# Strassen pairs of a down projection: T's weight sum on VectorE in place of transfers, all pairs one feed-forward block later, the product banks' folds moved back

## The chip, the cores and the metric

The kernel runs on one core of one Trainium2 chip. The metric is the device time of one execution in microseconds (us). The engines are TensorE (PE in the profile, with its weight loads as PEld), VectorE (DVE), ScalarE (ACT), GpSimd (POOL) and SyncE (SP). SP and POOL also issue transfers (DMAs) between HBM and SBUF; only POOL's transfers can add what they bring to what is already in SBUF.

## The reference

A trunk of two layers on one sequence of 256 tokens with 1024 features, all in float32. Each layer has a token mixer and a SwiGLU feed-forward network. The change lies in the feed-forward network of the second layer, which is the end of the program:

```
def swiglu(h, w13, w2):
    g, u = jnp.split(h @ w13, 2, axis=-1)
    return ((jax.nn.silu(g) * u) @ w2).astype(h.dtype)

for layer in range(DEPTH):
    ...
    h = h + y
    h = h + swiglu(rms_norm(h, norm_ffn[layer]), ffn_w13[layer], ffn_w2[layer])
return rms_norm(h, final_norm)
```

`w13` has 1024 rows and 2 x 2816 columns, `w2` has 2816 rows and 1024 columns. In blocks of 128, the hidden dimension of 2816 is 22 blocks.

## The kernel before

**Precision.** Float32 operands are handed to TensorE as two parts. ScalarE rounds a piece to its high part (`whi`, line 448, for weights), VectorE subtracts that from the piece to get the low part (`wlo`, line 450). A product is then three matmuls: high by high, high by low, low by high. A piece of weights is up to 128x1024 elements. These two instructions are called its split below. Products of activations (`xh`/`xl`, `hh`/`hl`) are split in the same way.

**Weights.** They are laid out ahead in one array, in the order in which they are used (`weight_plan`). SP loads a segment of 128x1024 (512 KB) into a ring of buffers called `raw`; two more buffers of this ring lie in the tile `bt`, which is free by then, so in this stage it holds 8.

**The feed-forward network of the second layer.** Block j (0 to 21) of the hidden dimension takes 48 matmuls (`gate_up`): 8 input blocks by gate and up by three. From block 4 on all of them write one PSUM bank, half gate, half up. `hidden1` then lets ScalarE apply silu to the gate half (`sgq`, line 1434) and VectorE multiply the up half by it (`uu`, line 1449; `u`, line 1455, for the last blocks). The next block may write that bank only after this.

**Strassen pairs.** The first 18 of 22 row blocks of the down projection are taken two at a time, in 9 pairs (`QUADS`), by Strassen's scheme: seven products in place of eight, each summed over all pairs in a PSUM bank of its own, `m7[1]` to `m7[7]` (1, 2, 3, 5 shown as psA, 4, 6, 7 as psB). The weights of a pair are two segments, a = [A | B] and b = [C | D]. Four pieces are made of them:

- "D" is A - B, a VectorE subtraction (`wdiff`, line 486);
- the plain piece is a itself;
- "S" is b + a, made by a POOL transfer of 512 KB that adds a's data from HBM into b's buffer (line 475);
- "T" is [A + D | B + C], made by two POOL transfers of 256 KB that add b's halves, swapped, into a's buffer, once a's own split has read it.

When the odd block of a pair is there, `combine` makes the four activation operands. `early(p)` then runs products 1, 2 and 5 (pieces D and a, 9 matmuls), `late(p)` products 3 and 4 (piece S) and 6 and 7 (piece T), 12 matmuls. Blocks 4 to 21 are followed by these halves in turn: block 4 + 2p by early(p), block 5 + 2p by late(p). The last 4 row blocks of the down projection are plain matmuls in `Final`, into four of the same banks, and then residual, norm and output.

**Folds.** After the last pair, VectorE adds each product bank into the result `ht` with the sign and place that Strassen's scheme gives it (`fold`, line 1500). All folds read and write `ht`, so they run in the order in which they were created: banks 2, 5, 5, 1, 1, 3, 4, 4. `Final`'s first part writes into bank 3, another into bank 2, each after that bank's fold.

**Order.** The program hands operations to a list scheduler with an engine, a cost and a due time, counted in tiles of TensorE's work. The scheduler sets each engine's order by these, and the engine then runs its instructions strictly in that order. The pieces of weights are made in the order of a list, `subs`; S and T of a pair are entered in it a given number of segments after the pair's own (`then`). A buffer that is `held` is not given back to its ring until its last split.

Of the kernel before, what the change touches and what calls it, by code (L numbers as in the profile page):

```python
# [16 lines left out]
S = 256  # L17
D = 1024
# [23 lines left out]
def weight_plan():  # L42
# [28 lines left out]
    def ffn(layer):  # L71
        for k in range(KT - 2):
            for j in range(4):
                plan.append(("ffn_w13", layer, k, P * j, P))
                plan.append(("ffn_w13", layer, k, DFF + P * j, P))
        for j in range(4):
            for half in range(2):
                column("ffn_w13", layer, half * DFF + P * j, (KT - 2, KT - 1))

        for j in range(4, FTN):  # L80
            column("ffn_w13", layer, P * j)
            column("ffn_w13", layer, DFF + P * j)
            if layer == 0:
                rows("ffn_w2", layer, j - 4)
            elif j % 2 == 0:
                plan.extend(quad(j - 4))
        if layer == 0:
            for k in range(FTN - 4, FTN - 2):
                rows("ffn_w2", layer, k)
            last_rows("ffn_w2", layer, FTN)  # L90
        else:
            for k in range(FTN - 4, FTN):
                for nh in range(2):
                    plan.append(("ffn_w2", layer, k, 512 * nh, 512))
# [216 lines left out]
def hybrid_trunk(ctx: ExitStack, tc: tile.TileContext, wts, xT, par, gfin, tab, onehot, masks, out):  # L311
# [98 lines left out]
    for si, (_, n) in enumerate(segs):  # L410
        if si in quads:
            add_sub("D", si, 0, 512, 2)
            add_sub("", si, 0, SUB, 4)
            then = [3, si]
        elif si - 1 not in quads:
            for o in range(0, n, grain(si)):
                m = min(grain(si), n - o)
                add_sub("", si, o, m, m // P)
        if then:
            then[0] -= 1  # L420
            if then[0] < 0:
                add_sub("S", then[1] + 1, 0, SUB, 4)
                add_sub("T", then[1], 0, SUB, 4)
                then = []
# [4 lines left out]
    def make_subs(upto):  # L429

        while ws["made"] < min(upto, len(subs)):
# [4 lines left out]
                quad_sums(si, due)  # L436
            elif kind == "" and o == 0 and si not in quads:
                load(si, due)
            src = {"": raws, "D": diffs, "S": raws, "T": raws}[kind][si]
            h = new("whi", [P, SUB], NSUB, FR, held=True)  # L440
            lo = new("wlo", [P, SUB], NSUB, FR, held=True)
            hi_b.append(h)
# [4 lines left out]
            else:  # L447
# [1 line left out]
                      reads=[src], alloc=[h], due=due)  # L449
            ov = od.op("V", cv(n), lambda h=h, lo=lo, r=src, o=o, n=n: V.tensor_tensor(  # L450
                lo[:, :n], r[:, o:o + n], h[:, :n].bitcast(FT), op=OP.subtract), reads=[src, h], alloc=[lo], due=due + .01)
            if not (kind == "" and si in quads):
                src.held = False
            else:
                add_rows(src, (0, 512), si + 1, (512, 0), due + 1)
            if i:
                oa.after, ov.after = ws["A"], ws["V"]
                ws["A"] = oa
# [6 lines left out]
        loads[si] = od.op("S", 60, lambda: nc.sync.dma_start(  # L465
            r[:, :m], wts[c0 // CHUNK, :, c0 % CHUNK:c0 % CHUNK + m]), alloc=[r], nbytes=m * 512, due=due)

    diffs = {}

    def add_rows(b, to, si, frm, due):  # L470

        n = segs[si][0] // CHUNK
        for t, f in ((to[0], frm[0]),) if to == frm else zip(to, frm):
            w = SUB if to == frm else 512
            o = od.op("G", 1000, lambda t=t, f=f, w=w: nc.gpsimd.dma_start(b[:, t:t + w], wts[n, :, f:f + w], accum_op=OP.add),  # L475
                      writes=[b], nbytes=1024 * w, due=due)
            o.deps += b.writers[:1]

    def quad_sums(si, due):

        load(si, due)
        load(si + 1, due)
        a, b = raws[si], raws[si + 1]
        d = diffs[si] = Buf(rings["wdiff"])
        a.held = b.held = True
        od.op("V", cv(512), lambda: V.tensor_tensor(d.tile, a[:, :512], a[:, 512:], op=OP.subtract), reads=[a], alloc=[d],
              due=due - 1)
        add_rows(b, (0, 512), si, (0, 512), due)

    class Piece:  # L490
        def __init__(self, i, c, n):
# [813 lines left out]
    def more_raws():  # L1305

        old, turn = rings["raw"], [0]

        def make():
            turn[0] += 1  # L1310
            n = (turn[0] - 1) % (RAW + 2)
            return bt.tile[:, D * (n + 1):D * (n + 2)] if n < 2 else old.make()
        rings["raw"] = Ring(make, RAW + 2)
        rings["raw"].past = [Buf(None), Buf(None)] + old.past[-RAW:]
    st3 = Stats()
    banks3 = [main_bank("A") for _ in range(4)]
    for k in range(KT):
# [177 lines left out]

    def fold(i, *to):

        for tt, nh, op in to:
            c = slice(512 * nh, 512 * nh + 512)
            read[i] = od.op("V", cv(512), lambda tt=tt, c=c, op=op: V.tensor_tensor(ht[:, tt, c], ht[:, tt, c], m7[i][:, :], op=op),  # L1500
                            reads=[m7[i], ht], writes=[ht], due=2)

    def early(p):
        x = ops[p]
# [5 lines left out]
        for t in "da":  # L1510
            x[t].free()
        if p == QUADS - 1:
            fold(2, (1, 1, OP.subtract))
            fold(5, (0, 1, OP.subtract), (0, 0, OP.add))
            fold(1, (0, 0, OP.add), (1, 1, OP.add))

    def late(p):
        x = ops[p]
# [1 line left out]
        product(p, 3, x["c"], 0, Piece(w.i, 512, 512))  # L1520
        product(p, 4, x["c"], 1, Piece(w.i, 0, 512))
        if p == QUADS - 1:
            fold(3, (1, 1, OP.add))
            fold(4, (0, 0, OP.add), (1, 0, OP.add))
        w = sub_piece("T", SUB)
        product(p, 6, x["b"], 0, Piece(w.i, 0, 512))
        product(p, 7, x["b"], 1, Piece(w.i, 512, 512))
# [8 lines left out]
    for j in range(4, FTN):  # L1536
# [7 lines left out]
        if j == 4:  # L1544
            od.op("A", ca(D), lambda: A.activation(gf.tile, gf.tile, AF.Copy, scale=2 * float(D) ** 0.5), reads=[bt],
                  writes=[gf], due=30)
        (late if j % 2 else early)((j - 4) // 2)
    for k in range(KT):
        x4[k].free()
    final.update({(0, 0): m7[7], (1, 0): m7[3], (0, 1): m7[2], (1, 1): m7[6]})  # L1550
# [4 lines left out]
    for tt in range(2):  # L1555
        fin = Final(tt)
        for i, (nh, o, n) in enumerate(FIN):
            b = final[nh, tt]
            if b in (m7[2], m7[3]):
                od.need(lambda: read[2 if b is m7[2] else 3].end)  # L1560
            for k in ks:
                p = w[k, nh]
                mm_x(b[:, o:o + n], hs[k], Piece(p.i, p.c + o, n), tt, stop=(k == FTN - 1), cost=n / 2.4 + 2.5)
# [54 lines left out]
```

## Time and profile before

| | us |
|---|---|
| three runs | 630.06, 634.36, 635.02 |
| their median | 634.36 |
| the profiled execution, its own time | 633.32 |
| its span in the profile | 631.6 |
| granted TensorE clock over the span | 0.991 |

The span runs from the first to the last instruction of the profiled execution; the 1.7 us beside it lie around it. Times in rows of the profile count from the span's start. The second layer's feed-forward blocks from block 4 on, and with them all that the change touches, lie from about 435 us on. Busy time says how long an engine had an instruction at work, not whether it held anyone up; for that the rows of waits and the chain of work that ended last are read, which name what released each engine. PEclk is the share of full clock that TensorE was granted.

### The profile page before, as it was taken

Reading aid. Unit: us, or ns where it says so; the run is one execution under the profiler, and the core shown is the slowest. Engines: PE = TensorE matmul, PEld = TensorE weight load, DVE = VectorE, ACT = ScalarE, POOL = GpSimd, SP = SyncE. Lnnn points to the kernel's source line nnn. Section 1 sums busy time; section 2 is a strip of 40 time slices with the busy share of each in tenths; the row PEclk is TensorE's granted clock in tenths of the full one; section 3 lists DMA queues with packets and bytes.
Section 4 is the critical chain, followed back from the end, with each engine's and each line's share of the span. In section 5 each row is a group of like instructions: output and inputs, shape, how many; then the busy total and the mean of one; then the engine's idle time right before and its main releaser. Section 6 shows DMA issues by size and latency. Waiting matters only on the chain.

```text
span 631.6 us, 12416 instructions
## 1 busy us (share of the span) xinstructions
PE 610.2 (97%) x4783; PEld 584.6 (93%) x4783; DVE 463.0 (73%) x852; ACT 381.6 (60%) x759; POOL 78.4 (12%) x128
## 2 busy tenths in 40 slices
PE   9999999999999999999999999999899999989985
PEld 7899999999999999999988999999899888988875
DVE  6899997877947666666695788766986666677673
ACT  6799989755635444444475666657855444455543
POOL 0052222000320000000001000004310111111102
PEclk9999999999999999999999999999989999989999
DMA  8855344543998555555526644476468786987911
GB/s 298 336 180 199 136 168 134 168 168 134 194 246 285 198 200 191 184 195 200 200 101 214 220 168 142 159 250 184 101 215 253 203 256 142 313 237 216 249 19 66
DMA packets 37142, 121.93 MB, mean 193 GB/s; under 512 B 4987, under 2 KB 6523, under 8 KB 37084
## 3 DMA queue, kind: packets, MB, share of 16 engines
q1 hardware_dynamic: 31484, 109.05, 50.0%
q0 software_dynamic: 4640, 11.34, 10.8%
q10 hardware_dynamic: 960, 0.76, 0.4%
q8 instruction: 37, 0.61, 0.4%
q14 instruction: 21, 0.17, 0.1%
HBM read 119.76 MB, written 1.38 MB: 192 GB/s over the span
## 4 chain that ended last, share of the span: by engine, by line
PE 59%; issue 25%; DMA 7%; DVE 5%; ACT 2%; POOL 1%; SPq 0%; DVEq 0%; ACTq 0%; POOLq 0%
PE psB L531 37%; PE psA L531 21%; DMA bt<-scr 3%; DVE wlo L450 3%; DMA raw<-in_w_dram 2%; ACT whi L448 1%; DMA bt<-in_w_dram 1%; DMA scr<-be 1%; POOL ny L705 0%; PE psB L1275 0%; ACT u L1414 0%; DVE uu L1449 0%; DVE xl L1419 0%; ACT sgq L1434 0%; POOL u L1416 0%
## 5 line engine op out<-in xcount | busy, mean ns | idle before, releaser
L450 DVE TENSOR_TENSOR wlo<-raw,whi 128x1024 fp32r<-128x1024 f32 (+1 forms) x199 | 237.9, 1206 | 84.1 <-ACT whi L448 84.1
L448 ACT ACTIVATE whi<-raw 128x1024 fp32r<-128x1024 f32 (+1 forms) x198 | 204.3, 1044 | 119.9 <-PE psA L531 49.6
L531 PE MATMUL psB<-xh,whi 128*128 128x256 f32 x608 | 173.7, 289 | 2.8 <-DVE uu L1449 2.8
L531 PE MATMUL psB<-xh,wlo 128*128 128x256 f32 x608 | 168.5, 280 | 0.0
L531 PE MATMUL psB<-xl,whi 128*128 128x256 f32 x608 | 164.0, 280 | 0.0
L531 PE MATMUL psA<-xh,whi 128*128 128x256 f32 x544 | 151.1, 281 | 0.0
L531 PE MATMUL psA<-xh,wlo 128*128 128x256 f32 x544 | 148.7, 277 | 0.0
L531 PE MATMUL psA<-xl,whi 128*128 128x256 f32 x544 | 143.6, 277 | 0.0
L531 PEld LDWEIGHTS psB<-xh,whi 128*128 128x128 f32 x608 | 115.7, 190 | 5.0 <-ACT hh L1464 3.2
L531 PEld LDWEIGHTS psB<-xh,wlo 128*128 128x128 f32 x608 | 115.5, 190 | 0.8 <-DVE wlo L450 0.3
L531 PEld LDWEIGHTS psB<-xl,whi 128*128 128x128 f32 x608 | 113.0, 191 | 0.0
L531 PEld LDWEIGHTS psA<-xh,whi 128*128 128x128 f32 x544 | 102.2, 188 | 0.2
L531 PEld LDWEIGHTS psA<-xh,wlo 128*128 128x128 f32 x544 | 102.3, 188 | 0.0
L531 PEld LDWEIGHTS psA<-xl,whi 128*128 128x128 f32 x544 | 99.1, 188 | 0.0
L1434 ACT ACTIVATE sgq<-psB 128x256 f32<-128x256 f32 x18 | 6.9, 384 | 61.8 <-PE psB L531 61.8
L531 PE MATMUL psB<-hl,whi 128*128 128x256 f32 x160 | 44.2, 276 | 0.0
L531 PE MATMUL psB<-hh,whi 128*128 128x256 f32 x160 | 44.2, 276 | 0.0
L531 PE MATMUL psB<-hh,wlo 128*128 128x256 f32 x160 | 44.2, 276 | 0.0
L475 POOL DMA_DIRECT2D raw<-in_w_dram x19 | 16.7, 1017 | 190.9 <-DMA bt<-in_final_dram 90.2
L705 POOL TENSOR_TENSOR ny<-nv,mhalf 128x2 f32<-128x2 f32 x5 | 6.5, 1297 | 215.1 <-DVE nv L702 192.6
L531 PEld LDWEIGHTS psB<-hh,whi 128*128 128x128 f32 x160 | 30.0, 188 | 0.0
L531 PEld LDWEIGHTS psB<-hh,wlo 128*128 128x128 f32 x160 | 30.0, 188 | 0.0
(242 smaller groups left out, 966.5 us busy)
## 6 DMA issues: line engine op xcount, KB each, us to landing
raw<-in_w_dram SPq DMA_DIRECT2D x187, 512.0 KB, 3.4
bt<-in_w_dram SPq DMA_DIRECT2D x15, 512.0 KB, 4.7
raw<-in_w_dram POOLq DMA_DIRECT2D x7, 512.0 KB, 9.8
raw<-in_w_dram POOLq DMA_DIRECT2D x12, 256.0 KB, 7.3
bt<-in_w_dram POOLq DMA_DIRECT2D x6, 256.0 KB, 5.4
hT<-in_x_dram SPq DMA_DIRECT2D x8, 128.0 KB, 4.8
raw<-in_w_dram SPq DMA_DIRECT2D x4, 256.0 KB, 4.8
bt<-scr POOLq DMA_DIRECT2D x16, 64.0 KB, 8.8
```

What stands on the lines that cost most here:

```text
L448: oa = od.op("A", ca(n), lambda h=h, r=src, o=o, n=n: A.activation(h[:, :n], r[:, o:o + n], AF.Copy), reads=[src], alloc=[h], due=due)
L450: ov = od.op("V", cv(n), lambda h=h, lo=lo, r=src, o=o, n=n: V.tensor_tensor(lo[:, :n], r[:, o:o + n], h[:, :n].bitcast(FT), op=OP.subtrac ...
L475: o = od.op("G", 1000, lambda t=t, f=f, w=w: nc.gpsimd.dma_start(b[:, t:t + w], wts[n, :, f:f + w], accum_op=OP.add), writes=[b], nbytes=1 ...
L531: T.matmul(o, a, b, start=start, stop=stop, skip_group_check=True)
L705: od.op("G", 500, lambda: G.tensor_tensor(y.tile, v.tile, mhalf, op=OP.pow), reads=[v], alloc=[y], due=due)
L1434: od.op("A", ca(S), lambda: A.activation(s.tile, b[:, :S], AF.Silu), reads=[b], alloc=[s], due=due)
```

## The change

T is now made by one VectorE addition of a and b, with the halves of b swapped, into a new buffer `wsum`, which lies in `bt`. It must read b before S's transfer adds into it, so that transfer now waits for the addition. The two POOL transfers of T are gone. Since `wsum` takes a place in `bt`, the ring `raw` has 7 buffers in place of 8.

Each pair comes one block later: early(p) after block 5 + 2p, late(p) after block 6 + 2p. The last half, late(8), follows early(8) at once, with no block between. The order of the weights follows, and S and T of the last pair are entered two segments sooner than those of the others.

The folds of the banks are created in the order 5, 5, 1, 1, 2, 3, 4, 4, with due times of 0 to 18 in place of 2 for all.

```diff
@@ weight_plan
-            elif j % 2 == 0:
-                plan.extend(quad(j - 4))
+            elif j % 2 and j > 4:
+                plan.extend(quad(j - 5))
@@ the list of pieces
-            then = [3, si]
+            then = [1 if quads[si] == FTN - 6 else 3, si]
@@ make_subs
-            src = {"": raws, "D": diffs, "S": raws, "T": raws}[kind][si]
+            src = {"": raws, "D": diffs, "S": raws, "T": sums}[kind][si]
...
-            if not (kind == "" and si in quads):
+            if kind != "D":
                 src.held = False
-            else:
-                add_rows(src, (0, 512), si + 1, (512, 0), due + 1)
@@ quad_sums
-        add_rows(b, (0, 512), si, (0, 512), due)
+        t = sums[si] = Buf(rings["wsum"])
+        t.held = True
+        halves = lambda t: t.rearrange("p (z c) -> p z c", z=2)
+        od.op("V", cv(SUB), lambda: V.tensor_tensor(halves(t.tile), halves(a.tile), cut(b, 512, (-512, 2), (1, 512)),
+                                                    op=OP.add), reads=[a, b], alloc=[t], due=due + 1)
+        c0 = segs[si][0]
+        od.op("G", 1000, lambda: nc.gpsimd.dma_start(b.tile, wts[c0 // CHUNK], accum_op=OP.add), writes=[b],
+              nbytes=2 * 524288, due=due + 1)
@@ more_raws
-            n = (turn[0] - 1) % (RAW + 2)
-            return bt.tile[:, D * (n + 1):D * (n + 2)] if n < 2 else old.make()
-        rings["raw"] = Ring(make, RAW + 2)
-        rings["raw"].past = [Buf(None), Buf(None)] + old.past[-RAW:]
+            return bt.tile[:, 2 * D:3 * D] if turn[0] % (RAW + 1) == 1 else old.make()
+        rings["raw"] = Ring(make, RAW + 1)
+        rings["raw"].past = [Buf(None)] + old.past[-RAW:]
+        inside("wsum", D, SUB, 1)
@@ fold: its due time is now given with each
-        for tt, nh, op in to:
+        for tt, nh, op, due in to:
...
+            read.setdefault(i, []).append(o)
@@ early
-            fold(2, (1, 1, OP.subtract))
-            fold(5, (0, 1, OP.subtract), (0, 0, OP.add))
-            fold(1, (0, 0, OP.add), (1, 1, OP.add))
+            fold(5, (0, 1, OP.subtract, 5), (0, 0, OP.add, 6))
+            fold(1, (0, 0, OP.add, 7), (1, 1, OP.add, 18))
+            fold(2, (1, 1, OP.subtract, 14))
@@ late
-            fold(3, (1, 1, OP.add))
-            fold(4, (0, 0, OP.add), (1, 0, OP.add))
+            fold(3, (1, 1, OP.add, 0))
+            fold(4, (0, 0, OP.add, 4), (1, 0, OP.add, 12))
@@ the loop over blocks
-        (late if j % 2 else early)((j - 4) // 2)
+        if j > 4:
+            (early if j % 2 else late)((j - 5) // 2)
+    late(QUADS - 1)
```

Three places show how this moves the instructions. In the rows, the name left of the arrow is written and those right of it are read; a number behind a name tells buffers of one name apart, and `bt_127` is the tile that holds `wsum` and part of the `raw` ring.

VectorE, around late(4). Before, first the product of hidden (`uu`) of block 12, then that of block 13, then its combinations and the split of T(4) (`wlo` from `bt_127`), which late(4) uses right after block 13:

```order
L1449 TENSOR_TENSOR uu_7251<-psB_6344,sgq_7240 128x256
L486 TENSOR_TENSOR wdiff_7265<-raw_7204 128x512
L1449 TENSOR_TENSOR uu_7251<-psB_6344,sgq_7306 128x256
L1473 TENSOR_TENSOR be_2493<-uu_7251 128x128
L1476 TENSOR_TENSOR sgq_7315<-uu_7251 128x256
L1480 TENSOR_TENSOR u_7318<-uu_7251 128x256
L450 TENSOR_TENSOR wlo_7323<-bt_127,whi_7310 128x1024
L450 TENSOR_TENSOR wlo_7331<-raw_7137,whi_7320 128x1024
L1465 TENSOR_TENSOR hl3_7346<-be_2493,hh3_7333 128x128
L1465 TENSOR_TENSOR hl4_7348<-sgq_7315,hh4_7335 128x256
```

VectorE now, around the same late(4), which follows block 14. It begins in the middle of the combinations of block 13; the splits from `bt_127` are S(4) and then T(4), the two after them are of gate and up weights, `uu_7408` is the product of block 14, and the addition into `bt_127` is T(5)'s:

```order
L1461 TENSOR_TENSOR hl4_7331<-sgq_7308,hh4_7321 128x256
L450 TENSOR_TENSOR wlo_7346<-bt_127,whi_7323 128x1024
L1461 TENSOR_TENSOR hl6_7354<-u_7317,hh6_7336 128x256
L450 TENSOR_TENSOR wlo_7361<-bt_127,whi_7341 128x1024
L450 TENSOR_TENSOR wlo_7377<-raw_7222,whi_7356 128x1024
L450 TENSOR_TENSOR wlo_7391<-raw_7239,whi_7372 128x1024
L475 TENSOR_TENSOR wdiff_7401<-raw_7272 128x512
L1445 TENSOR_TENSOR uu_7408<-psB_6344,sgq_7403 128x256
L480 TENSOR_TENSOR bt_127<-raw_7272,raw_7274 128x1024
L450 TENSOR_TENSOR wlo_7423<-wdiff_7401,whi_7416 128x512
```

T's split stood behind the product of the block that late follows at once; it now stands ahead of the product of the next block, which late follows. The sum of the next pair's T, a new instruction, stands behind that product.

POOL, at the start of block 4's inputs, which are eight multiplications (`u`). Before, with the transfer of S(0) first:

```order
L475 DMA raw_6005<-in_w_dram 128x1024
L705 TENSOR_TENSOR ny_6115<-nv_6109,mhalf_108 128x2
L1416 TENSOR_TENSOR u_6146<-u_6146,rrow_6140 128x256
L1416 TENSOR_TENSOR u_6148<-u_6148,rrow_6140 128x256
L1416 TENSOR_TENSOR u_6154<-u_6154,rrow_6140 128x256
L1416 TENSOR_TENSOR u_6213<-u_6213,rrow_6140 128x256
```

POOL now, with `in_w_dram` the array of weights:

```order
L701 TENSOR_TENSOR ny_6099<-nv_6095,mhalf_108 128x2
L1412 TENSOR_TENSOR u_6136<-u_6136,rrow_6120 128x256
L1412 TENSOR_TENSOR u_6144<-u_6144,rrow_6120 128x256
L1412 TENSOR_TENSOR u_6148<-u_6148,rrow_6120 128x256
L1412 TENSOR_TENSOR u_6189<-u_6189,rrow_6120 128x256
L483 DMA raw_6132<-in_w_dram 128x1024
L1412 TENSOR_TENSOR u_6225<-u_6225,rrow_6120 128x256
L1412 TENSOR_TENSOR u_6235<-u_6235,rrow_6120 128x256
```

S(0)'s transfer stood ahead of these multiplications and now stands behind the fourth of the eight.

VectorE, at the end. Before, from the splits ahead of block 21's product (`u_8091`) to the last split; a fold adds a psA or psB bank into `ii`, the name under which the result lies, and the banks here are 3 (psA_6545) and 4 (psB_6552):

```order
L450 TENSOR_TENSOR wlo_8074<-bt_127,whi_8062 128x1024
L450 TENSOR_TENSOR wlo_8081<-raw_7907,whi_8067 128x1024
L1455 TENSOR_TENSOR u_8091<-psB_6344,sgq_8077 128x256
L1500 TENSOR_TENSOR ii_6069<-ii_6069,psA_6545 128x512
L1500 TENSOR_TENSOR ii_6069<-ii_6069,psB_6552 128x512
L1465 TENSOR_TENSOR hl4_8106<-u_8091,hh4_8100 128x256
L1500 TENSOR_TENSOR ii_6069<-ii_6069,psB_6552 128x512
L450 TENSOR_TENSOR wlo_8110<-raw_7930,whi_8083 128x1024
L450 TENSOR_TENSOR wlo_8113<-raw_7962,whi_8088 128x1024
L450 TENSOR_TENSOR wlo_8118<-bt_127,whi_8103 128x1024
```

VectorE now, from T(8)'s split, which stands right behind block 21's product, to the fold of bank 3 (psA_6634); the folds before it are of banks 5 (psA_6553), 1 (psA_6529) and 2 (psA_6538):

```order
L450 TENSOR_TENSOR wlo_8069<-bt_127,whi_8058 128x1024
L1461 TENSOR_TENSOR hl4_8080<-u_8063,hh4_8073 128x256
L450 TENSOR_TENSOR wlo_8083<-raw_7937,whi_8065 128x1024
L1496 TENSOR_TENSOR ii_6063<-ii_6063,psA_6553 128x512
L450 TENSOR_TENSOR wlo_8095<-raw_7967,whi_8077 128x1024
L1496 TENSOR_TENSOR ii_6063<-ii_6063,psA_6553 128x512
L450 TENSOR_TENSOR wlo_8099<-raw_7983,whi_8086 128x1024
L1496 TENSOR_TENSOR ii_6063<-ii_6063,psA_6529 128x512
L450 TENSOR_TENSOR wlo_8102<-bt_127,whi_8093 128x1024
L1496 TENSOR_TENSOR ii_6063<-ii_6063,psA_6529 128x512
L1496 TENSOR_TENSOR ii_6063<-ii_6063,psA_6538 128x512
L1496 TENSOR_TENSOR ii_6063<-ii_6063,psA_6634 128x512
```

Bank 3's fold stood ahead of the last three splits, with five folds done before block 21's product; it now stands behind that product, four 1024 wide splits after T's, and all folds of banks 5, 1 and 2.

More of the change, by code (lines that the diff above doesn't have):

```diff
@@ L466, in load @@
             r[:, :m], wts[c0 // CHUNK, :, c0 % CHUNK:c0 % CHUNK + m]), alloc=[r], nbytes=m * 512, due=due)
[L468 to L477, printed above, removed]
+    diffs, sums = {}, {}
     def quad_sums(si, due):
@@ L1496, in fold @@
     def fold(i, *to):
-        for tt, nh, op in to:
+        for tt, nh, op, due in to:
             c = slice(512 * nh, 512 * nh + 512)
-            read[i] = od.op("V", cv(512), lambda tt=tt, c=c, op=op: V.tensor_tensor(ht[:, tt, c], ht[:, tt, c], m7[i][:, :], op=op),
-                            reads=[m7[i], ht], writes=[ht], due=2)
+            o = od.op("V", cv(512), lambda tt=tt, c=c, op=op: V.tensor_tensor(ht[:, tt, c], ht[:, tt, c], m7[i][:, :], op=op),
+                            reads=[m7[i], ht], writes=[ht], due=due)
+            read.setdefault(i, []).append(o)
     def early(p):
@@ L1559, in hybrid_trunk @@
             if b in (m7[2], m7[3]):
-                od.need(lambda: read[2 if b is m7[2] else 3].end)
+                od.need(lambda: read[2 if b is m7[2] else 3][0].end)
             for k in ks:
```

## The prediction

> **What bounds the kernel now.** I read the page first, then busy time by stretches cut where a pair's second half starts on TensorE, then the waits and the timeline at one such start, then the chain of waits, and last the transfers. Early(p) and late(p) are the two halves of Strassen pair p.
>
> ```profile
> span 631.6 us, 12416 instructions
> PE 610.2 (97%) x4783; PEld 584.6 (93%) x4783; DVE 463.0 (73%) x852; ACT 381.6 (60%) x759; POOL 78.4 (12%) x128
> ```
>
> TensorE is the bound at 97%, and the change takes no product away. It can gain only where TensorE waits, and that is the last third. Rows below: window, its length, busy time of PE, PEld, DVE, ACT, POOL, granted clock, DMA share, GB/s.
>
> ```profile
> core 0: us, PE busy (x) PEld busy (x) DVE busy (x) ACT busy (x) POOL busy (x), PEclk, DMA share, GB/s
> 434.68:465.62 30.94, 28.11 (x218) 27.40 (x217) 25.28 (x47) 21.97 (x42) 10.15 (x11) 0.94 0.51 139
> 465.62:481.36 15.74, 15.74 (x120) 14.88 (x118) 10.07 (x16) 7.50 (x12) 2.61 (x3) 1.00 0.91 263
> 481.36:497.78 16.42, 16.42 (x119) 15.25 (x118) 10.95 (x17) 8.22 (x13) 2.64 (x3) 1.00 0.78 211
> 497.78:515.54 17.76, 16.58 (x119) 14.91 (x118) 12.09 (x18) 9.05 (x14) 2.62 (x3) 1.00 0.88 267
> ...
> 551.26:570.89 19.63, 17.86 (x119) 16.10 (x118) 12.26 (x18) 9.28 (x14) 2.62 (x3) 0.91 0.92 250
> ...
> 588.84:606.35 17.51, 16.72 (x120) 15.19 (x119) 15.60 (x19) 10.78 (x14) 1.76 (x2) 1.00 0.64 165
> 606.35:631.60 25.25, 16.18 (x86) 13.55 (x84) 12.02 (x27) 10.75 (x23) 4.79 (x5) 0.90 0.11 42
> ```
>
> Each row but the first and the last is one period, from late(p) to late(p+1). The first two hold the same matmuls as the rest and keep TensorE wholly busy; their mean, 16.08 us, is what a period costs without waits. The six that begin with late(2) to late(7) take 606.35 - 497.78 = 108.57 us, 18.10 each. The excess sits in late itself: windows from late's first matmul to the next block's first, for late(1) and late(2).
>
> ```profile
> 481.36:484.10 2.74, 2.74 (x14) 2.26 (x13) 1.42 (x2) 2.48 (x4) 0.00 (x0) 1.00 0.96 342
> 497.78:502.28 4.50, 3.33 (x15) 2.19 (x13) 3.85 (x8) 4.30 (x9) 0.00 (x0) 1.00 0.69 179
> ```
>
> Late(1) takes 2.74 us, late(2) 4.50. What it waits for there, by the row of waits (us in all, times, longest; TensorE's waits from late(2) to late(7)) and by the timeline (start, length, engine, in brackets the idle time before and what ended it):
>
> ```profile
> PE psB L531 <- DVE wlo L450: 5.7, 6, 1.1
> ...
> 497.98 0.38 ACT L1434 ACTIVATE sgq<-psB 128x256 f32<-128x256 f32 x1 [7.38 <-PE psB L531]
> 498.26 1.05 ACT L448 ACTIVATE whi<-raw 128x1024 fp32r<-128x1024 f32 x1
> 498.40 0.42 DVE L1449 TENSOR_TENSOR uu<-psB,sgq 128x256 f32<-128x256 f32 x1 [4.78 <-ACT sgq L1434]
> 499.74 1.22 DVE L450 TENSOR_TENSOR wlo<-raw,whi 128x1024 fp32r<-128x1024 f32 x1
> 501.01 0.50 PE L531 MATMUL psB<-wlo,hh 128*128 128x512 f32 x1 [1.15 <-DVE wlo L450]
> ```
>
> T's split (498.26 and 499.74) is queued behind the silu of the block that has just ended, though ScalarE had stood idle 7.38 us and VectorE 4.78. T's sum had landed; order made it late. Only at late(5) the transfer itself ended last:
>
> ```profile
> 542.73 9.87 DMA raw<-in_w_dram
> ...
> 552.71 1.07 ACT whi L448
> ```
>
> **The part that gains.** One block later, a whole gate and up block stands between the hidden work that T's split follows and T's use. Prices (a group's length over its count; of back-to-back work, from one start to the next):
>
> ```profile
> 523.88 3.49 DVE L450 TENSOR_TENSOR wlo<-raw,whi 128x1024 fp32r<-128x1024 f32 x3
> 601.15 2.60 DVE L1500 TENSOR_TENSOR ii<-ii,psA 128x512 f32<-128x512 f32 x4
> ...
> 563.53 2.06 PE psA L531 x9
> 565.59 5.48 PE psB L531 x48
> 621.07 2.76 PE psA L531 x12
> ```
>
> So a 1024 wide VectorE operation costs (3.49 - 1.22)/2 = 1.14 us, a fold about 0.64; early takes 2.06, a block 5.5, late 2.76. Set late(p) at 0: late ends at 2.8, the odd block at 8.3, early at 10.3, the even block at 16.08, where late(p+1) starts. VectorE meets the odd block's hidden work at 8.9, works on it until about 11, splits S until 12.3 and T until 13.9 (two operations of 0.34 stand between). TensorE wants T's low half at 16.08 + 1.6, 3.8 us later. The waits of late go: 6 x (18.10 - 16.08) = **-12.1 us**. If every period took 16.42 it is 10.1, if 15.74, 14.2. The excess of late(2) alone, 4.50 - 2.74 = 1.76, six times is 10.6; late(5), with its transfer and the half clock (0.91 in its row), lost more.
>
> T's sum on VectorE: no row shows it; the nearest are the splits of the same shape, two inputs from SBUF, 1.14 us. That makes VectorE 12.2 + 1.1 = 13.3 of 16.08 us. Its cover is VectorE's idle time; without it each sum would cost at most 1.14 x 9 = 10.3. I take 0. The 18 half transfers of T leave POOL's queue and the DMA engines; since just late(5) waited for one, this adds nothing. The ring of 7 in place of 8 makes SP's loads wait for S's split; a load needs 6.3 us (below) and its block starts 14 us after that split, so 0.
>
> S is the new risk. Its transfer now waits for T's sum, which stands behind the even block's hidden product: from 0.6 to 0.95, sum done at 2.1. Its landing, by rows of POOL: 5.4 with nothing of T in the queue (at 426), then, in late(2) to late(8), S behind T's halves, T's halves, and SP's loads:
>
> ```profile
> raw<-in_w_dram POOLq DMA_DIRECT2D x1, 512.0 KB, 5.4
> ...
> raw<-in_w_dram POOLq DMA_DIRECT2D x4, 512.0 KB, 9.6
> raw<-in_w_dram POOLq DMA_DIRECT2D x8, 256.0 KB, 8.5
> raw<-in_w_dram SPq DMA_DIRECT2D x25, 512.0 KB, 6.3
> ```
>
> I take 5.4 to 7.5, nearest the row without T: landed by 9.6, and ScalarE reaches it at about 9.7. Then 0. In pair 1 S's split even precedes the hidden product of block 7, with 0.2 to spare: **+0.2** (0 to 0.9).
> The Trainium skill (DMA: Bandwidth & Descriptors, Anatomy of one DMA - SWDGE path) fits 2.0 us + bytes/436e3, by which an S transfer would be 3.2 us and the last rival below impossible. The rows disagree, 5.4 at the least, so that rival keeps its chance.
>
> **The part that costs, the start.** Block 5 may start when VectorE has read block 4's bank:
>
> ```profile
> 448.06 0.41 DVE L1449 TENSOR_TENSOR uu<-u,sgq 128x256 f32<-128x256 f32 x1
> 457.88 0.42 DVE L1449 TENSOR_TENSOR uu<-psB,sgq 128x256 f32<-128x256 f32 x1
> 458.45 0.35 PE L531 MATMUL psB<-xh,whi 128*128 128x256 f32 x1 [2.83 <-DVE uu L1449]
> ```
>
> Before, early(0) fills 2.06 us of that stall. Now it follows block 5, while VectorE has about as much to do between these two products (24 instructions then, 25 now: a 1024 split less, a 512 split and two small ones more). POOL takes S(0)'s issue between the eight multiplications that feed block 4, about 1 us later, and the sums of squares are 11 matmuls (1.3 us) earlier; I let these cancel. So **+2.1** (1 to 3.3).
>
> **The tail.** Block 21 now comes before early(8) and late(8), 4.8 us of cover. But the folds depend on each other in program order, 5, 5, 1, 1, 2, 3, 4, 4, and the first Final part writes into bank 3, so it waits for bank 3's fold.
>
> ```profile
> 606.54 0.39 ACT L1434 ACTIVATE sgq<-psB 128x256 f32<-128x256 f32 x1 [1.78 <-PE psB L531]
> 606.96 0.42 DVE L1455 TENSOR_TENSOR u<-psB,sgq 128x256 f32<-128x256 f32 x1 [0.76 <-ACT sgq L1434]
> 609.11 0.28 PE L531 MATMUL psA<-whi,hh 128*128 128x256 f32 x1
> ...
> 614.44 3.81 PE psB L531 x12
> 618.25 1.41 PE psA L531 x12
> ```
>
> Before: block 21 ends at 606.35, late(8) until 609.11, the first part lasts to 614.3 where 1.41 is needed: 3.8 lost. After, from the block's end: product of hidden at 0.6 to 0.95, T's split until 2.65, a small one until 3.15 (it waits for ScalarE), four splits and six folds until 3.15 + 4 x 1.14 + 6 x 0.64 = 11.6. TensorE is there at 4.8: 6.8 lost. **+3.0** (2 to 5, the top if S(8), whose sum stands behind two splits, is late). The lowered clock after the stall costs 3.81 - 2.76 = 1.05 now. A stall nearly twice as long can bring more, up to the 0.10 x 25.25 = 2.5 that the whole last window lost: **+0.4** (0 to 1.5).
>
> **Sum**, against the profiled execution's own 633.3 us (span 631.6; the median of the runs is 634.4, 1.1 above): 633.3 - 12.1 + 0.2 + 2.1 + 3.0 + 0.4 = **626.9**.
>
> **Rivals.** (1) The free periods are like the first, 15.74, and the start hides early(0): 633.3 - 14.2 + 1 + 2 + 0.2 = 622. For it: that row; against it: the next, 16.42. (2) Colder restarts: both stalls, 4.9 and 6.8 us, are longer than any shown, and after the 2.83 us one the clock was 0.94 over 30.94 us, 1.9 us lost. One more such loss: 628.8, with the stalls' upper ends 631. The Trainium skill (TensorE: Matmul & The Clock Gate, Part 1) has the clock halved after an idle window of 3.4 us and freed after a busy one. By that rule both restarts are cold, while the trace shows that a shorter stall suffices. (3) T's wait only changes its name, because VectorE at 13.3 of 16.08 falls behind at each hidden product: 0.5 to 1.1 back in nine periods, 632 to 637. Against it: 3.8 us of slack. (4) The other side: S lands late. In VectorE's order T's sum of the next pair follows S's split, T's, two more, wdiff and the hidden product: landing + 1.05 + 4 x 1.14 + 0.7 + 0.6 + 0.35 + 1.14 = landing + 8.4 is a ring that must fit in 16.08. It decides from a landing of 7.7 us; each us more costs seven periods 1 us. From 8.8 the kernel is no faster (634.6), from 9.7 slower by over 1%; at 9.6 it is 640. For it: the 9.6 row; against it: T's halves, which stood ahead, are gone.
>
> **Chances.** Forecast 0.48 (own range 624 to 630), (1) 0.13, (2) 0.14, (3) 0.08, (4) 0.17, 0.10 of it from a landing of 9.7 on. About 1% is what a measurement of this kernel can tell from no change; faster then means under 628.0, slower over 640.7. Two thirds of the forecast's 0.48, all of (1) and 0.03 of (2) lie under: 0.48. Slower: 0.10 from (4). The rest, 0.42, is the same. Range 621 to 636: from below (1)'s 622 to near the end of (3); it leaves out (4) from 9.1 on, 0.13, and some 0.04 of (1) and (3).
>
> **What would show it.** Periods of 15.7 to 16.5 with TensorE busy throughout and the hidden product's bank never waited for; a stall of some 4.9 us before block 5, no half clock until the tail; S landing in 5 to 7.5 us; a stall of 6 to 8 us before Final, ended by a fold. Wrong if late still waits for wlo, if S's landings near 8 us push the even block's product, or if the tail waits for splits rather than a fold.

## The result

| | before | after |
|---|---|---|
| median of 20 runs (us) | 632.62 | 627.75 |
| lowest and highest | 629.23 to 636.62 | 625.79 to 631.92 |
| profiled execution, its span | 631.6 | 625.9 |

The ratio is 0.9931, with a 95% interval of 0.9910 to 0.9952: faster, by 0.7%. The forecast was 626.9 in a range of 621 to 636, so the number came out about as forecast: the sum went from 633.3 us down by 6.4, the medians differ by 4.9, the profiled spans by 5.7. By the 1% that the prediction took as the least to tell from no change, 0.7% is still "the same". The experiments below show that the reason given for it did not hold: the move of the pairs, which was to bring the gain, costs, and T's sum on VectorE, which was entered at nothing, brings all of it.

**The profile after.** The page first, and TensorE's waits from block 4's inputs on (what waited, for what: us in all, times, longest):

```profile
span 625.9 us, 12406 instructions
PE 603.5 (96%) x4783; PEld 583.1 (93%) x4783; DVE 474.8 (76%) x861; ACT 382.8 (61%) x759; POOL 62.5 (10%) x110
```

```profile
PE psA L527 <- DVE ii L1496: 7.4, 1, 7.4
PE psB L527 <- DVE uu L1445: 5.6, 2, 4.8
PE psB L527 <- DVE u L1436: 0.9, 1, 0.9
```

TensorE is busy for as many instructions as before. Before, its waits were for weights (`wlo`) in nearly every pair; none is left. In their place stand one wait for a fold (7.4 us), one for block 4's product of hidden (4.8, where it was 2.8 before), and two short ones. The windows show where they lie. Columns as before; the first row ends where block 5 starts, the second is block 5, then periods from late(p) to late(p+1) for p = 0, 1, 4, 5 and 6, and last the tail from the end of late(8):

```profile
433.51:459.17 25.66, 20.02 (x174) 19.67 (x171) 22.49 (x44) 21.03 (x41) 9.23 (x9) 0.95 0.49 147
459.17:466.71 7.54, 7.54 (x48) 7.54 (x49) 5.01 (x6) 1.65 (x2) 0.00 (x0) 0.72 0.59 208
474.24:489.98 15.74, 15.74 (x119) 14.88 (x118) 12.35 (x18) 8.88 (x13) 0.90 (x1) 1.00 0.71 225
489.98:505.72 15.74, 15.74 (x119) 14.88 (x118) 12.12 (x19) 9.29 (x14) 0.86 (x1) 1.00 0.72 217
...
537.20:552.94 15.74, 15.74 (x119) 14.88 (x118) 11.16 (x18) 8.75 (x14) 0.86 (x1) 1.00 0.81 261
552.94:569.75 16.81, 16.00 (x120) 14.80 (x118) 15.45 (x22) 9.96 (x15) 0.87 (x1) 1.00 0.73 229
569.75:585.49 15.74, 15.74 (x120) 14.88 (x118) 12.90 (x16) 8.79 (x12) 0.87 (x1) 1.00 0.84 260
599.09:625.90 26.81, 13.07 (x73) 11.80 (x72) 14.22 (x30) 8.32 (x20) 4.78 (x5) 0.84 0.11 39
```

All periods but one are 15.74 us with TensorE busy throughout; the six before took 18.10 each. From the start of block 5 to the end of late(8) it is 599.09 - 459.17 = 139.92 us now, 609.11 - 458.45 = 150.66 before, although early(0), 2.06 us, now falls into it: 10.7 us less. Block 5 starts 0.7 us later. The tail takes 26.81 us in place of 631.60 - 609.11 = 22.49: 4.3 more. 0.7 - 10.7 + 4.3 gives the -5.7 of the spans.

The one longer period, at late(5), is S arriving late. First S(5)'s transfer (issued at 540.38, us to landing at the end of the row), then the start of its split on ScalarE and the block that follows late(5) on TensorE, each with the idle time before it, and what ended that, in brackets:

```profile
raw<-in_w_dram POOLq DMA_DIRECT2D x1, 512.0 KB, 8.4
```

```profile
548.86 1.06 ACT L448 ACTIVATE whi<-raw 128x1024 fp32r<-128x1024 f32 x1 [1.95 <-DMA raw<-in_w_dram]
556.66 0.39 PE L527 MATMUL psB<-xh,whi 128*128 128x256 f32 x1 [0.81 <-DVE uu L1445]
```

The ring that the prediction wrote down for this case, landing + 8.4, gives 8.4 + 8.4 = 16.8 us from one issue of S to the next. The next one, S(6)'s, came at 558.27, so the ring took 17.9 us, 1.1 more than its prices gave. That TensorE's period is 16.81 is chance: it is 16.00 us of work and the wait of 0.81.

The tail, by the chain of work that ended last (start, length, what):

```profile
587.34 6.37 DMA raw<-in_w_dram
...
593.82 1.07 ACT whi L448
...
594.91 1.23 DVE wlo L450
...
604.90 0.70 DVE ii L1496
...
605.70 0.70 DVE ii L1496
606.39 0.14 issue
606.53 2.90 PE psA L527 x12
```

S(8) is issued at 587.34 and lands at 593.71. VectorE had nothing in reach until its split at 594.91 (that instruction shows 5.47 us of idle time before it). Then it works without a pause through block 21's product, T's split, four splits for `Final` and six folds, the last of them bank 3's, done at 606.39. TensorE has been through with late(8) since 599.09 and waits 7.4 us.

### The profile page after: what moved, and what is told of

Its sections match the earlier page's. It is cut to its first block, busy times and chain, and to the rows that moved or that the text cites. A ratio compares the mean times of both kernels' runs of the same rounds, so it can differ in the third digit from the quotient of the medians.

```text
span 625.9 us, 12406 instructions
## 1 busy us (share of the span) xinstructions
PE 603.5 (96%) x4783; PEld 583.1 (93%) x4783; DVE 474.8 (76%) x861; ACT 382.8 (61%) x759; POOL 62.5 (10%) x110
## 5 line engine op out<-in xcount | busy, mean ns | idle before, releaser
L527 PEld LDWEIGHTS psB<-hl,whi 128*128 128x128 f32 x160 | 30.0, 188 | 0.0
```

Source lines behind the costliest of these rows:

```text
L527: T.matmul(o, a, b, start=start, stop=stop, skip_group_check=True)
```

## The experiments

They ran in three groups, each together with the kernel before on one chip; ratios are to that kernel's runs in the group, with 95% intervals. Its medians there were 632.38, 632.21 and 632.72 us.

**T's sum alone.** The kernel before with `quad_sums`, the source of T's split and the ring as after the change; pairs, weights' order and folds as before.

```diff
-            src = {"": raws, "D": diffs, "S": raws, "T": raws}[kind][si]
+            src = {"": raws, "D": diffs, "S": raws, "T": sums}[kind][si]
...
+        od.op("V", cv(SUB), lambda: V.tensor_tensor(halves(t.tile), halves(a.tile), cut(b, 512, (-512, 2), (1, 512)),
+                                                    op=OP.add), reads=[a, b], alloc=[t], due=due + 1)
```

> The kernel before, with T's sum by VectorE into its own buffer and a ring of 7, but with the pairs and the folds where they were. Theory 1 (what held late up was only that T's split stood behind the product of the block that late follows; the transfers put it there): in this order T's split already stands ahead of that product, so the waits for wlo go without the move: periods of 15.7 to 16.1 us in place of 18.1, the start and the tail as before, 10 to 13 us less than before. Theory 2 (a block of distance is needed, since S, which now waits for T's sum, must land and be split within one block): late waits for S's or T's split instead, periods stay at 17 us or more, and the time is within 4 us of before.

Measured: 616.48 us, ratio 0.9756 (0.9730 to 0.9781), more than three times the gain of the whole change. TensorE's waits, and windows of block 5, of the stretch from 0.7 us into late(2) to the start of late(8), of one period, and of the tail:

```profile
PE psB L527 <- DVE uu L1445: 3.5, 2, 3.0
PE psA L527 <- DVE ii L1496: 1.1, 1, 1.1
```

```profile
458.28:465.51 7.23, 7.23 (x48) 7.23 (x49) 6.80 (x8) 1.68 (x2) 0.12 (x1) 0.76 0.75 235
498.65:594.87 96.22, 96.22 (x701) 90.94 (x699) 79.78 (x111) 55.54 (x82) 4.33 (x6) 1.00 0.72 208
514.10:530.25 16.15, 16.15 (x119) 15.25 (x118) 13.49 (x19) 9.29 (x14) 0.86 (x2) 1.00 0.80 225
597.63:616.60 18.97, 11.55 (x73) 10.22 (x72) 8.49 (x24) 6.46 (x18) 4.79 (x5) 0.91 0.15 55
```

TensorE is busy for all of the 96.22 us: without the move late waits for nothing. Theory 1 held for the loop, and block 5 starts as before (458.28). The gain is 3 us above its 10 to 13, because the tail, which it had as before, falls from 22.5 to 19.0 us: in VectorE's order T(8)'s split and three of `Final`'s four now stand ahead of block 21's product. With T's transfers gone S(1) to S(8) also land in 5.3 to 7.3 us, where they took 7.4 to 10.2 before; what share of the gain that has, no run separates.

**The move alone.** The changed kernel with T by POOL's two transfers again.

```diff
-            src = {"": raws, "D": diffs, "S": raws, "T": sums}[kind][si]
+            src = {"": raws, "D": diffs, "S": raws, "T": raws}[kind][si]
...
+            else:
+                add_rows(src, (0, 512), si + 1, (512, 0), due + 1)
```

> The changed kernel with T by POOL's two transfers again (ring of 8): the move and the folds alone. Theory 1: in this order T's split again stands behind the product of the block that late follows, so late waits as before (periods of 17 us or more), while the costs of start and tail stay: 3 to 8 us slower than before. Theory 2 (the distance of a block does it): periods of 15.7 to 16.4, and the time of the changed kernel, 4 to 6 us less than before. Beside it, on why blocks took 5.5 to 5.9 us before and 5.47 after the change: if T's transfers slow the matmuls, blocks without a wait take 5.6 and more here, if not, 5.47.

Measured: 635.81 us, ratio 1.0062 (1.0041 to 1.0082): slower. Waits, and three periods:

```profile
PE psB L531 <- DVE uu L1449: 7.3, 2, 6.2
PE psB L531 <- DVE wlo L450: 6.2, 7, 1.7
```

```profile
489.75:505.49 15.74, 15.74 (x119) 14.88 (x118) 9.55 (x16) 6.32 (x11) 2.65 (x3) 1.00 1.01 298
505.49:522.63 17.14, 16.27 (x119) 14.78 (x118) 12.23 (x18) 9.45 (x14) 2.65 (x3) 1.00 0.87 248
522.63:539.73 17.10, 16.30 (x120) 14.80 (x118) 12.24 (x18) 9.46 (x14) 2.66 (x3) 1.00 0.84 254
```

Late waits for `wlo` as before (of the 7.3 us for `uu`, 6.2 are the stall before block 5). A block of distance did not help, because the split moved with it: it stands behind the product of the block that late now follows.

**Order alone.** The same kernel, with T's transfers planned as if they took no time on the wire; the planner then puts T's split ahead of that product. No instruction is added or taken away.

```diff
-                      writes=[b], nbytes=1024 * w, due=due)
+                      writes=[b], nbytes=1024 * w if w == SUB else 0, due=due)
```

> The kernel with the move and T's two transfers, but planned as if they took no time on the wire, so that T's split is put ahead of the product of the block that late follows; the work is the same. Theory 1 (the place in VectorE's order is what made late wait; the transfers land early enough after the move): late's waits for wlo of 0.8 us each go, periods fall from 17.0 to 17.2 to 15.7 to 16.3, and the time falls by 4 to 8 us to 628 to 632. Rival (the transfers themselves are too slow, 8 to 11 us to land behind one another): VectorE now waits for them ahead of that product, blocks are held up in its place, periods stay at 16.8 us or more, and the time is within 3 us of the move alone (635.8) or above it.

Measured: 639.22 us, ratio 1.0102 (1.0077 to 1.0128). Waits, the start of T(3)'s split on ScalarE, and the landings of POOL's transfers over the loop:

```profile
PE psB L531 <- DVE uu L1449: 10.8, 4, 6.0
PE psB L531 <- DVE u L1455: 3.0, 1, 3.0
```

```profile
522.22 1.06 ACT L448 ACTIVATE whi<-raw 128x1024 fp32r<-128x1024 f32 x1 [5.46 <-DMA raw<-in_w_dram]
```

```profile
raw<-in_w_dram POOLq DMA_DIRECT2D x7, 512.0 KB, 9.2
raw<-in_w_dram POOLq DMA_DIRECT2D x12, 256.0 KB, 7.3
```

The rival held. No wait for `wlo` is left; the blocks wait for the products instead (10.8 us, 6.0 of them before block 5, and 3.0), which stand behind splits that wait for transfers, as T(3)'s does. From late(2) to late(7) the periods run from 15.74 to 20.7 us, 18.3 in the mean, where the move alone has 17.6. `Final` waits 7.8 us for a fold here. So the place in the order was not the cause by itself. T's transfers start only after a's split and land 7.3 us later (median), ahead of or behind S's, which takes 9.2. Whichever place the split is given, something waits for it.

**The folds.** The changed kernel with the folds in the old order and with the old due time.

```diff
-            fold(5, (0, 1, OP.subtract, 5), (0, 0, OP.add, 6))
-            fold(1, (0, 0, OP.add, 7), (1, 1, OP.add, 18))
-            fold(2, (1, 1, OP.subtract, 14))
+            fold(2, (1, 1, OP.subtract))
+            fold(5, (0, 1, OP.subtract), (0, 0, OP.add))
+            fold(1, (0, 0, OP.add), (1, 1, OP.add))
```

> The changed kernel with the folds created in the old order (2, 5, 5, 1, 1, 3, 4, 4) and with the old due time. Theory 1 (bank 3's fold ends last because of what stands ahead of it, six folds and four splits in both orders): Final's wait stays at 7.4 us within 0.7, the time within 1 us of the changed kernel, so 4 to 6 less than before. Rival (the moved folds save time at the tail): the wait is longer by 1 us or more, and the time is 3 less than before or worse.

Measured: 628.08 us, ratio 0.9931 (0.9905 to 0.9957), the same as the whole change. `Final`'s wait is 7.3 us against 7.4. Within these intervals the moved folds neither help nor harm: in both orders bank 3's is the sixth.

**The tail.** The changed kernel with early(8) after block 20, behind late(7), so that block 21 stands between it and late(8); the order of the weights follows.

```diff
-        if j > 4:
+        if 4 < j < FTN - 1:
             (early if j % 2 else late)((j - 5) // 2)
+        if j == FTN - 2:
+            early(QUADS - 1)
     late(QUADS - 1)
```

> The changed kernel with the last pair's first half, early(8), after block 20 again, so that block 21 stands between it and late(8); S(8) is then issued a block sooner. Theory 1 (Final waits 7.4 us because S(8) lands late, VectorE idles for 5.5 us, and bank 3's fold ends a queue of splits and folds that starts only then): the wait falls to 3 to 4.5 us, the whole to 2.5 to 4.5 us less than the changed kernel, 7 to 10 less than before. Rival (the queue of splits for Final sets the end, whatever S does): the wait stays at 6 us or more, and the gain over the changed kernel is under 1.5 us.

Measured: 624.19 us, ratio 0.9872 (0.9848 to 0.9896). Waits before and in `Final`:

```profile
PE psA L529 <- DVE wlo L452: 2.5, 3, 1.4
PE psA L529 <- DVE ii L1498: 1.0, 1, 1.0
```

Theory 1 held: 7.4 us became 3.5, and the kernel is 3.6 us faster than the changed one by the medians. In the profiled executions it is 3.4: 2.7 at the tail and 1.2 in the loop, where late(5) did not wait for S, less 0.4 at the start. What set the wait was that S(8) landed so late that all of VectorE's last work stood behind it.

**The start.** The changed kernel with early(0) after block 4; the order of the weights follows.

```diff
-        if j > 4:
+        if j == 4:
+            early(0)
+        elif j > 5:
             (early if j % 2 else late)((j - 5) // 2)
```

> The changed kernel with the first pair's early(0) after block 4 again (late(0) stays after block 6). Theory 1 (the start costs because early(0) no longer fills the stall before block 5, which is set by VectorE): block 5 starts at the same time within 0.7 us, the stall falls from 4.8 to about 2.8 us, and the kernel is 1.5 to 3 us faster than the changed one, so 6 to 8 us less than before. Rival (early(0) brings its weight splits with it ahead of the product of block 4 and delays it by as much): the stall stays above 4 us after early(0), no gain.

Measured: 624.14 us, ratio 0.9880 (0.9855 to 0.9906), 3.6 us faster than the changed kernel. Waits:

```profile
PE psA L529 <- DVE ii L1498: 7.2, 1, 7.2
PE psB L529 <- DVE uu L1447: 3.9, 2, 2.9
```

The stall before block 5 is 2.9 us again, with early(0) ahead of it. In the profiled executions the gain is 2.9: block 5 starts 0.8 us sooner, the stretch from there to the end of late(8) is 2.8 shorter (early(0)'s 2.06, and late(5), which did not wait for S in this one, less a new wait of 0.99 us before block 6), and the tail is 0.7 longer.

**Both ends.** early(0) after block 4 and early(8) after block 20 together, so that the move is left in the middle only; the order of the weights follows.

```diff
-        if j > 4:
+        if j == 4:
+            early(0)
+        elif 5 < j < FTN - 1:
             (early if j % 2 else late)((j - 5) // 2)
+        if j == FTN - 2:
+            early(QUADS - 1)
     late(QUADS - 1)
```

> The changed kernel with early(0) after block 4 and early(8) after block 20 again, so that only the middle keeps the move. Theory 1 (the two ends each cost what was found for them, and the move gains nothing beside T's sum): the gains add, 8 us of the changed kernel's wait and 2 to 3 more, 617 to 622 us on the scale where before is 632.4, not faster than T's sum alone. Rival (the move gains in the middle what it loses at the ends): with the ends undone it is 2 us or more faster than T's sum alone, 614 or less.

Measured: 622.44 us, ratio 0.9838 (0.9812 to 0.9864), 0.4 above the band of theory 1 and 6 us slower than T's sum alone. The rival fell: even with its ends undone the move gains nothing. It can't, since with T's sum on VectorE late waits for nothing in either place. The middle still moves late(7) one block nearer to the tail, where VectorE has the splits and folds for `Final` to do. The tail of this run:

```profile
598.33:622.43 24.10, 14.72 (x72) 12.34 (x72) 11.22 (x26) 7.43 (x19) 4.77 (x5) 0.78 0.12 44
```

It takes 24.10 us against 18.97 in T's sum alone, 5.1 of the 5.8 between the two spans. TensorE waits in it for `wlo` (2.5 us) and a fold (0.5), where T's sum alone waits 1.1 for a fold; the other 3.2 us are the same matmuls at a lower granted clock (0.78 against 0.91), which keep TensorE busy for 14.72 us against 11.55.

**The stall at the start, with T's sum alone.** The combinations of blocks 2 and 3 are due later, so that block 4's product stands six instructions earlier on VectorE.

```diff
-        due = 6
+        due = 30 if p == 1 else 6
         ops[p] = {t: X("h", (4 * p + n) % 7) for n, t in enumerate("dacb")}
```

> T's sum alone on VectorE (pairs and folds as before), with the combinations of blocks 2 and 3 due later, so that the product of block 4 stands six instructions earlier in VectorE's order. Theory 1 (the 3.0 us stall before block 5 is VectorE's queue, and a shorter stall also leaves the clock up): block 5 starts 1 to 2 us earlier, the stall is under 2 us, and the kernel is 1 to 4 us faster than T's sum alone. Rival (ScalarE's silu or the weights end the stall): block 5 starts within 0.4 us of where it did, no gain.

Measured: 627.19 us, ratio 0.9916 (0.9895 to 0.9936), 11 us slower than T's sum alone: a miss for both theories. The start did what theory 1 said (block 5 at 457.01, a stall of 1.4 us, clock 1.00 in the block behind it). But late waits again, for the splits of S (of the 6.6 us in the first row, the longest and a second wait, 2.4 together, lie in `Final`):

```profile
PE psA L527 <- DVE wlo L450: 6.6, 8, 1.9
PE psA L527 <- ACT whi L448: 2.0, 4, 1.3
PE psB L527 <- DVE uu L1445: 1.4, 1, 1.4
```

The planner had moved more than the six instructions. T's sum of every pair had slid from ahead of the odd block's product to some ten rows behind it, and S is issued only after that sum. S(4)'s issue in T's sum alone, where late(4) starts at 530.25, and here, where it starts at 527.16:

```profile
513.71 0.86 POOL L483 DMA_DIRECT2D raw<-in_w_dram  x1 [15.04 <-DVE bt L480]
```

```profile
519.15 0.86 POOL L483 DMA_DIRECT2D raw<-in_w_dram  x1 [16.57 <-DMA raw<-in_w_dram]
```

16.5 us ahead of its use there, 8.0 here, with 5 to 8 us to land and the two splits to come.

**The start with the sum held in place.** As the last one (by an early due time of block 4's product), and A - B, T's sum and S's issue due 9 tiles earlier than in T's sum alone.

```diff
-        due = 4
+        due = -20 if j == 4 else 4
...
-              due=due - 1)
+              due=due - 10)
...
-                                                    op=OP.add), reads=[a, b], alloc=[t], due=due + 1)
+                                                    op=OP.add), reads=[a, b], alloc=[t], due=due - 8)
...
-              nbytes=2 * 524288, due=due + 1)
+              nbytes=2 * 524288, due=due - 8)
```

> T's sum alone on VectorE (pairs and folds as before), with the product of block 4 put earlier in VectorE's order as in combine1_later, but with T's sum kept ahead of the odd block's product by an earlier due time. Theory 1 (combine1_later won about 3 us at the start and lost 10 to 12 later only because T's sum had slid behind two products, so that S landed 1 to 2 us ahead of its use): S is issued some 16 us before its use, late's waits are gone, block 5 starts near 457.0 with no lowered clock behind it, and the kernel is 2 to 4 us faster than T's sum alone: 612 to 615 on the scale where before is 632.3. Rival (the later combinations are what delayed the middle): late still waits 0.8 us or more in the middle, 620 us or more.

Measured: 612.70 us, ratio 0.9688 (0.9664 to 0.9713), the fastest here. Waits, block 5, and the stretch from late(0) to late(8):

```profile
PE psB L527 <- DVE uu L1445: 1.4, 1, 1.4
PE psA L527 <- DVE ii L1496: 1.3, 1, 1.3
```

```profile
457.57:463.13 5.56, 5.56 (x48) 5.56 (x49) 5.56 (x11) 2.94 (x5) 0.00 (x0) 1.00 0.70 242
463.13:589.15 126.02, 126.02 (x939) 118.91 (x937) 109.17 (x153) 75.08 (x112) 6.92 (x8) 1.00 0.75 222
```

Nearly the same start, and a loop without a wait. So the place of T's sum in VectorE's order, which sets how early S starts, was what the run before had lost.

**The sum's due times in the changed kernel.**

```diff
-              due=due - 1)
+              due=due - 10)
...
-                                                    op=OP.add), reads=[a, b], alloc=[t], due=due + 1)
+                                                    op=OP.add), reads=[a, b], alloc=[t], due=due - 8)
...
-              nbytes=2 * 524288, due=due + 1)
+              nbytes=2 * 524288, due=due - 8)
```

> The changed kernel with T's sum due earlier, so that it and S's issue stand ahead of the product of the even block in VectorE's order, and T(8)'s split ahead of the product of block 21. Theory 1 (S lands with little to spare in the changed kernel, and its late landing costs at late(5) and above all before Final): no wait for a product in the middle, Final's wait falls from 7.4 to 4.5 to 6.5 us, the kernel is 1.5 to 3.5 us faster than the changed one: 624 to 626. Rival (the queue of folds and splits for Final alone sets the wait): the wait stays at 7 us or more, gain under 1 us.

Measured: 628.43 us, ratio 0.9939 (0.9916 to 0.9963), no gain over the change. `Final`'s wait fell to 5.4 us as theory 1 had it, but not because S(8) came sooner: it landed at 594.45, against 593.71 in the changed kernel. The wait is shorter because late(8) ended 2.7 us later. TensorE waited 2.2 us for products in the middle (0.8 in the changed kernel), and some periods without a wait ran slower. In the longest of these waits, 1.6 us, block 19's product stands behind S(7)'s split, and that split waited for a transfer that took 8.1 us.

In this run `Final` starts 12.8 us after S(8) lands (607.27 - 594.45). It does so in the changed kernel (12.8) and in the runs with early(0) back (12.8) and with the old folds (12.7), too. With T's sum on VectorE and late(8) right behind early(8), the landing of S(8) is what sets when `Final` starts, whatever the order of the folds.

## Why the prediction came out as it did

- **The late waits, -12.1.** The size was right: the six periods from late(1) to late(7) take 585.49 - 489.98 = 95.5 us, 13.1 less than the six before, although late(5) lost 1.1. Some of that is luck: the free periods ran at 15.74 us, rival (1)'s figure; six at the 16.15 of T's sum alone would be 11.7 less than before. The cause was wrong. The step that failed is "One block later, a whole gate and up block stands between the hidden work that T's split follows and T's use". The move alone leaves the waits in place (1.0062), and T's sum alone removes them (0.9756).
- **T's sum, "I take 0".** As a cost this was right: one sum takes 1.22 us, and no wait for it shows in T's sum alone. But "since just late(5) waited for one, this adds nothing" was the second half of the same error. The profile of before showed T's split queued behind a product, and the prediction took that place for the cause ("order made it late"). It was itself a consequence, since the planner had put the split where it expected the transfer to land. Given another place, with the transfers kept, VectorE waits for them (1.0102). The profile of before could have told: the prediction says "Only at late(5) the transfer itself ended last", but at late(3) T's split waits for it as well. Its second transfer, issued at 507.0, lands after 9.3 us, 0.8 us after late(3) has started at 515.54:

```profile
raw<-in_w_dram POOLq DMA_DIRECT2D x1, 256.0 KB, 9.3
```

```profile
516.42 2.01 ACT L448 ACTIVATE whi<-raw 128x1024 fp32r<-128x1024 f32 x2 [0.29 <-DMA raw<-in_w_dram]
```

  For pairs 2 to 7 that transfer lands 0.5 us ahead of late's start, 0.8 behind, 3.0 ahead, 1.3 behind, 0.3 ahead and 0.4 behind. A split takes 2.3 us (1.05 and 1.22), and late wants its result 1.6 us after its start, so by this estimate only pair 4's landed early enough for another order to free late.
- **The start, +2.1 (1 to 3.3).** Block 5 starts 0.7 us later and early(0)'s 2.06 comes on top: 2.8. Putting early(0) back showed the mechanism.
- **The tail, +3.0 and +0.4.** Together 3.4, measured 4.3, within the ends of the two terms. It was to be a wait for bank 3's fold, 6.8 us, and was 7.4. The queue was named rightly; S(8)'s landing, which the prediction had kept as the upper end, set where the queue began.
- **S.** Taken as 5.4 to 7.5 us, it landed in 6.1 (median of seven, with 6.9 for the one into `bt`). In the one period where a landing passed 7.7, rival (4) did come: TensorE lost 1.1 us there, though the ring itself took 17.9 us where its prices gave 16.8. By the fit in the Trainium skill (DMA: Bandwidth & Descriptors, Anatomy of one DMA - SWDGE path) the estimate is 3.2 us; the rows disagree in every run, with 5.2 us at the least.
- **VectorE at 13.3 of 16.08 us** had room: its busy time is 11.2 to 13.7 in the periods without a wait. The rival that it falls behind did not come.

The forecast came out close because both parts were in the change and their sum was worked out from the periods; that the gain was put down to the wrong part could not show in it, and this is luck. Of the parts, the one credited with the gain costs about 11 us by the medians (627.75 against 616.48). In the profiled executions it is 625.9 - 616.6 = 9.3: 7.8 at the tail (26.81 against 18.97) and 2.9 at the start, less 1.5 in the middle, where this change's profile ran at the faster of two paces (last section).

## What to carry to other kernels

A wait whose cause is read as "queued behind X" has a second question: why does it stand there? Where a planner chose the place, the operand's planned arrival may have set it, and then moving the consumer moves the queue with it; making the operand available sooner (here an addition of 1.2 us in place of two transfers that land after some 8) frees both. A change of several parts is costed by each part alone as well as together, since a sum can be right with the parts' signs exchanged. And a due time moved for one instruction can shift others by a dozen places: compare the whole order before reading the time.

## What the runs showed of the hardware

- **The clock after a stall.** Blocks behind a TensorE stall, in three profiles (1.64 us in the changed kernel with the sum due earlier, 1.84 in the one with the old folds, and this change's 4.78, its row above):

```profile
583.08:588.64 5.56, 5.56 (x49) 5.56 (x49) 5.56 (x7) 2.93 (x4) 0.00 (x0) 1.00 0.58 188
```

```profile
486.44:493.74 7.30, 7.30 (x49) 7.30 (x50) 7.17 (x12) 2.69 (x6) 0.00 (x0) 0.77 0.49 152
```

  The granted clock stayed at 1.00 after 1.64 us, and fell to 0.77 after 1.84 and 0.72 after 4.78, at a cost of 1.7 to 2.1 us each. The Trainium skill (TensorE: Matmul & The Clock Gate, Part 1) has an idle window of about 3.4 us for it; here a stall of a little over half of that was enough. The length of one stall does not settle it alone: before, two waits of 1.01 and 0.76 us within 2.3 us brought the clock down at late(5) (0.91 in the prediction's row from 551.26), while two of 1.27 and 0.76 us within 2.5 us in the run with later combinations left it at 1.00.
- **Two paces of the same matmuls at the same clock.** A period of 119 or 120 matmuls without any wait took 15.74 us in this change's profile and 16.15 in that of T's sum alone, both at a granted clock of 1.00. It is not T's transfers: the move alone, which has them, shows 15.74 too. The run with the old folds, with the same loop as this change, ran it at the slower pace for most of its way. What sets it stays open; over 14 to 17 blocks it is worth 2 to 3 us, which lies within the spread of the runs.
